# Scan of a two-layer hybrid backbone: row halves issued in turn, one accumulation group for the output, and a step order by tile shape

## The chip, the cores and the metric

One NeuronCore of one Trainium2 chip. The metric is the device time of one execution in microseconds (us): the median of three executions before the change was 3622.27 us (3619.68 to 3623.23).

## The reference, cut to what matters

The program is a two-layer backbone over 1024 latent and 256 context tokens of 1024 channels. The change touches only one stage of layer 0: the two recurrences of the mixer, both in both directions of time.

```python
# eight RWKV-7 heads, state 64x64
S_t = S_{t-1} (diag(w_t) - kk_t (kk_t*a_t)^T) + v_t k_t^T ; y_t = S_t r_t
# four gated DeltaNet heads, state 128x128
S_t = e^{g_t} S_{t-1} + beta_t k_t (v_t - e^{g_t} S_{t-1}^T k_t)^T, o_t = S_t^T q_t
```

Each runs over the context tokens first and then, from that state, over the latent tokens, forwards and backwards. Around it lie the input projection, the output projection, a mixture of experts, and a second layer with windowed attention; all of these stay as they are.

## The kernel before, in words

Time is cut into chunks of 64 tokens, 20 of them (`NCH`), and a step `n` of `Scan.run` (L1142) handles one chunk of both directions and of all heads. All products are fp32, and the trace counts two matmul instructions (with two weight loads) for each product of the program.

Products are small, so each uses only a part of TensorE's 128x128 array. The profile prints that part as rows*columns, and this text calls it the tile shape. Two products in different parts of the array with the same shape can be under way together: in most loops the inner index (`hp`, the half of the heads, or `d`, the direction) selects partitions 0 to 63 or 64 to 127.

A step is made of generators whose pieces ("slices", one per `yield`) are interleaved by the string `ORDER` (L1178), one letter a slice:

- `r`, `rwkv(n)` (L1017): `ps_u` (shape 128*64, L1028), `ps_U` (64*64, L1036), `ps_S` (128*64, L1044), and the output `ps_y` in two slices. The output adds two products for each of 8 units `u`: one with `sv` and `qn` (128*64, L1063) and one with the state `S` (64*64, L1066). They stand one behind the other unit by unit, each unit its own accumulation group.
- `n`, `gdn(n)` (L1077): `ps_ks` and `ps_qs` (128*64, L1096), `ps_Y` (64*64, L1109), the new state `ps_Sg` of each direction in a slice of its own (64*128, L1119), and the output `ps_o` (64*64, L1130).
- `g`, `gram(n+1)` (L945): four slices of `ps_g` (64*128, L964), one for each pair of row half `hp` and direction `d`, each followed by two masks on VectorE (L966 into `ar`, L968 into `qn`); then two slices of transposes `ps_bk` (128*128, L975), copied by ScalarE.
- `c`, `corner(n+1)` (L979): six slices of `ps_p` (32*32, L989, L1003, L1005).

`g` and `c` make matrices of the next step that do not wait for the state. PSUM tiles rotate: three banks for `g` and `c` together (`psg`), two for `r`, three for `n`. TensorE, VectorE and GpSimd run in the order in which the program is written; ScalarE's order is a scheduler's.

The loads of a step come from SyncE's queue in program order: `load2` (L886) brings the channel operands of two steps at once (`ar`, `bk`, `kq`; double buffered), `load_tri` (L912) the inverses of step n+2 (`l21`, `t1`, `TT`), and `load_tok` (L928) the token operands `sv` and `at` of step n+2, behind the last slice of step n, into the buffer of step n. GpSimd gathers `kvtok`, stores `s_y` and `s_o`, and multiplies `dec` and `kd`. At step 6 (`LATER`) the queue also takes the 4 MB of the output projection's weights (`wo_raw`, L1291). In steps 0 and 1, VectorE also finishes a set of inverses (`tri_inv`, L796, L821 and L822), one slice per letter of `ORDER`.

```python
            for i, x in enumerate(ORDER if n else ORDER[1:]):
                if x in g:
                    next(g[x], None)
                if n or i >= TRI0:
                    tri.step(TRI)
```

Of the kernel before, what the change touches and what calls it, by code (L numbers as in the profile page):

```python
# [31 lines left out]
def step_of(m):  # L32
    """Step at which direction 1 meets chunk m, and the chunk of a step."""
    return 3 - m if m < 4 else 23 - m
# [6 lines left out]
def rows_ap(t, off, rows, cols):  # L41
    """rows x cols view of a contiguous DRAM tensor, from element `off`."""
    return bass.AP(tensor=t.tensor, offset=t.offset + off, ap=[[cols, rows], [1, cols]])
# [12 lines left out]
def log_exp_table(K):  # L56
    """Loads the activation table that serves Ln and Exp together."""
    K.table = K.tc.keep_in_program_order(K.nc.scalar.preload_act_table_set("natural_log_exp_and_others")).ins


def behind(K, ins, name):
    """Keeps an instruction behind the named one in program order."""
# [4 lines left out]
def after_table(K, ins):  # L67
    """Keeps an activation behind the last explicit table load."""
# [5 lines left out]
class Fill:  # L74
    """Generators advanced beside a main stream, one slice at a time; lead: instructions they are moved forward."""
# [26 lines left out]
# ---------------------------------------------------------------- constants  # L102
# [4 lines left out]
def consts(K, A):  # L107
# [9 lines left out]
    # per 64-row half: free index minus row index of the half  # L117
# [48 lines left out]
    # silu(c), silu(c_ctx) as [128 d, k, 32] stationaries with two live columns  # L166
# [6 lines left out]
# ---------------------------------------------------------------- ada modulation  # L173
def ada_part(K, A, layer, jj, wp, pp, wtag="adaw", ptag="adap", bufs=2):
    """N-chunks 4jj..4jj+3 of layer's modulation rows: rows 32g (lat), 32g+1 (ctx) of modr[:, jj]."""
# [37 lines left out]
def modcol(K, layer, m, kt, s):  # L213
    """[128,1] column of modulation m for channels 128kt.., stream s (0 lat, 1 ctx)."""
    g = (m % 2) * 2 + kt // 4
    return K.modT[layer][:, m // 2, kt % 4, g, s:s + 1]


def mod_bcast(K, layer, m, s, dst):
    """dst [128, D] <- modulation m of stream s on every partition."""  # L220
# [6 lines left out]
def norm_cols(K, pool, layer, norm, ms, mh, tag):  # L227
    """[128, 2, kt, stream]: gain * (1 + scale), shift of a modulated norm; ms, mh: scale and shift modulations."""
# [11 lines left out]
# ---------------------------------------------------------------- layer-0 input: norm, modulate, transpose  # L240
def head(K, A, hp, hh, hl):
    """hh + hl = modulated RMS norm of [ctx; x], channel layout [128, 8, T]."""
# [61 lines left out]
# ---------------------------------------------------------------- layer-0 projection, column tile by column tile  # L304
def both(nc, out, ps, func, **kw):
    """Activation of a projected column tile (context, latent) into token order."""
# [4 lines left out]
class InProj:  # L311
    """Projected column tiles (first column, continuation), weights loaded two tiles ahead across runs."""
# [28 lines left out]
    def run(self, posts, fills, drain):  # L341
        """Continues the next tiles with posts; fills: (generators, slices per k tile); drain: those to finish."""
# [23 lines left out]
def post_z(K, j, wk, tag, bufs):  # L366
    """Stores the silu of gate tile j."""
# [9 lines left out]
# ---------------------------------------------------------------- RWKV-7 operands  # L377
def store_L(K, unit, n0, x, rev=False):
    """x [(half, s), chunk, t] -> K.s_L [unit, chunk, half, s, t]; chunks n0.. (descending if rev)."""
# [3 lines left out]
class Rwkv:  # L383
    """Token shift, loras, decays and the chunk operands alpha, rho, beta, kappa of both directions.

    With c the running sum of the log decay inside a chunk, in the direction's order:
    alpha = kk e^(c-), rho = r e^c, beta = b e^-c, kappa = k e^-c.
    """
# [26 lines left out]
    def shift(self, ps, j, out):  # L415
        """out = (1 - mu) p + mu/2 (previous + next), zero beyond the ends of each stream."""
# [29 lines left out]
    def invert(self, ct):  # L446
        """Queues the inverses of a column tile once its chunk matrices are traced."""
# [5 lines left out]
    def prep_gen(self, ct):  # L453
# [14 lines left out]
        for bi, (a, m) in enumerate(BLK):  # L468
# [75 lines left out]
            # bonus and gate  # L544
# [28 lines left out]
# ---------------------------------------------------------------- gated DeltaNet operands  # L573
class Gdn:
    """Short convolution, gates and the chunk matrices of the gated delta rule, keys and queries not normalised.

    With nk = 1/|k|: L[t,s] = (k_t.k_s) e^(g_t-g_s) nk_s^2 beta_s, A[t,s] = (q_t.k_s) e^(g_t-g_s) nk_s^2 beta_s,
    r = v/nk - e^g S k, Y = (I+L)^-1 r, o = q S e^g + A Y, S' = e^(gl) S + (k nk^2 beta e^(gl-g))^T Y.
    Rows 0-63 carry direction 0, rows 64-127 direction 1 in flipped token order.
    """  # L580
# [12 lines left out]
    def to_chunks(self, ps, src, w):  # L593
        """ps [(d, p), step, w] <- src [128 token, tile, d, w], direction 1 flipped."""
# [20 lines left out]
    def gates(self, ab):  # L615
# [11 lines left out]
        # softplus(x) = max(x, 0) + ln(1 + e^-|x|)  # L627
# [33 lines left out]
    def conv(self, ps, j):  # L661
        """Five-tap centred convolution over tokens of column tile j."""
# [40 lines left out]
    def sums(self, sq, s, h):  # L703
        """K.ssq[tok, tile, s, h] = sum over channels of the squares, plus eps."""
# [23 lines left out]
    def tok(self, x, h, c0, scaled):  # L728
        """Channel tile x -> token rows of K.s_kv [T, 1024], columns of head h (values divided by nk)."""
# [60 lines left out]
# ---------------------------------------------------------------- inverses of the 32-blocks of I + L  # L790
def inv_blocks(K, c0):
    """The tensor of the inverses of chunk c0, its number of chunks and the place of c0 in it."""
# [1546 lines left out]
```

## Time and profile before

| | us |
|---|---|
| median of three executions | 3622.27 |
| lowest and highest | 3619.68, 3623.23 |
| span of the profiled execution, first to last instruction | 3620.5 |
| TensorE busy in that span | 3343.5 |
| VectorE, ScalarE, GpSimd busy | 2421.4, 2073.4, 731.6 |
| scan, start of step 2 to start of step 19 | 370.45 |

The page gives no separate time of the profiled execution; the median lies 1.8 us above its span. A row of the trace gives start, busy time, engine, line, operation, tiles, and, for a matmul, the tile shape; in square brackets stands the idle time of that engine before it and what ended it. Busy time is the union of a group, and the ends of matmuls are modelled, so the distance from one start to the next tells more than a busy time.

### The profile page before, as it was taken

The page shows a single profiled execution, that of the slowest core. Times are in us where ns is not written, and L with a number is a line of the kernel's source. Part 1 is how long each engine was busy: PE and PEld are TensorE (multiplying, and loading weights), DVE is VectorE, ACT ScalarE, POOL GpSimd, SP SyncE. Part 2 cuts the span into 40 slices and gives each one's busy share as a digit, 9 for nine tenths or more (in the row PEclk, how much of TensorE's full clock was granted, in tenths as well). Part 3 has the DMA queues.
Part 4 walks back from the last instruction along what each step waited for, and adds up shares of the span by engine and source line. Part 5 has one row for each costly group of instructions (what it writes and reads, how often), then busy time and mean ns, then how long its engine had stood idle before and what let it go on. Part 6 is the DMA issues. An engine that isn't in the chain of part 4 may idle for free. (4 is left out here: it accounts for less than half of the span.)

```text
span 3620.5 us, 60293 instructions
## 1 busy us (share of the span) xinstructions
PE 3343.5 (92%) x23392; PEld 2475.0 (68%) x23392; DVE 2421.4 (67%) x4034; ACT 2073.4 (57%) x3529; POOL 731.6 (20%) x716
## 2 busy tenths in 40 slices
PE   5999999996999979699999999899899986999997
PEld 3866667775888867566666666567667764888885
DVE  4267774667343356967777777644666588999998
ACT  4244554332333356376666666453577745888886
POOL 1233322222322244111111100101223310101001
PEclk8999999996999989899999999999699997999998
DMA  5255565666897756468888887663311138999995
GB/s 190 70 190 172 183 204 172 225 187 126 172 210 162 162 167 209 152 245 282 282 288 278 284 286 265 202 230 123 77 39 44 47 110 306 378 396 386 394 375 217
DMA packets 480161, 767.80 MB, mean 212 GB/s; under 512 B 231836, under 2 KB 318532, under 8 KB 472708
## 3 DMA queue, kind: packets, MB, share of 16 engines
q1 hardware_dynamic: 434640, 601.05, 50.2%
q0 software_dynamic: 41648, 151.55, 13.5%
q10 hardware_dynamic: 3587, 11.36, 1.0%
q8 instruction: 184, 3.01, 0.3%
q14 instruction: 102, 0.83, 0.1%
HBM read 631.48 MB, written 132.38 MB: 211 GB/s over the span
## 5 line engine op out<-in xcount | busy, mean ns | idle before, releaser
L1185 DVE TENSOR_TENSOR ulo<-raw,uhi 128x1024 fp32r<-128x1024 f32 x768 | 901.6, 1222 | 127.6 <-ACT uhi L1184 118.9
L1184 ACT ACTIVATE uhi<-raw 128x1024 fp32r<-128x1024 f32 x768 | 789.4, 1069 | 245.2 <-PE ps_y L1624 127.0
L1573 PE MATMUL ps_h<-uhi,xh 128*128 128x512 f32 x1024 | 333.7, 404 | 1.4 <-ACT uhi L1184 1.3
L1573 PE MATMUL ps_h<-ulo,xh 128*128 128x512 f32 x1024 | 320.4, 393 | 3.0 <-DVE ulo L1185 1.0
L1573 PE MATMUL ps_h<-uhi,xl 128*128 128x512 f32 x1024 | 319.0, 392 | 0.0
L1640 POOL DMA_INDIRECT s_x<-yo,idxl x31 | 49.2, 1587 | 977.1 <-DVE yo L1636 977.1
L1573 PEld LDWEIGHTS ps_h<-uhi,xh 128*128 128x128 f32 x1024 | 184.0, 188 | 73.5 <-ACT uhi L1184 21.4
L1573 PEld LDWEIGHTS ps_h<-ulo,xh 128*128 128x128 f32 x1024 | 190.6, 188 | 54.9 <-DVE ulo L1185 12.4
L1573 PEld LDWEIGHTS ps_h<-uhi,xl 128*128 128x128 f32 x1024 | 191.2, 188 | 41.5
L354 PE MATMUL ps_in<-hl,whi 128*128 128x512 f32 x512 | 172.2, 411 | 0.0
L354 PE MATMUL ps_in<-hh,wlo 128*128 128x512 f32 x512 | 169.4, 409 | 1.5 <-POOL wlo L338 1.5
L354 PE MATMUL ps_in<-hh,whi 128*128 128x512 f32 x512 | 169.5, 408 | 0.9 <-DVE convu L671 0.9
L1624 PE MATMUL ps_y<-uhi,th 128*128 128x512 f32 x512 | 167.2, 407 | 0.6 <-ACT tc L1610 0.5
L1624 PE MATMUL ps_y<-ulo,th 128*128 128x512 f32 x512 | 161.1, 395 | 0.1
L1624 PE MATMUL ps_y<-uhi,tl 128*128 128x512 f32 x512 | 158.7, 391 | 0.0
L1910 DVE CUSTOM_DVE_ANT_0 pe<-ps_s,amask,sink 128x640 f32<-128x640 f32 (+2 forms) x128 | 104.4, 816 | 66.7 <-PE ps_s L1903 65.0
L966 DVE TENSOR_TENSOR ar<-ps_g,strict 64x256 f32<-64x256 f32 x80 | 33.8, 422 | 154.2 <-PE ps_g L964 153.9
L1923 POOL TENSOR_SCALAR pe<-pe,ast 128x640 f32<-128x640 f32 (+1 forms) x48 | 92.1, 1919 | 215.1 <-DVE ast L1922 193.7
L1546 ACT ACTIVATE xv<-ps_x,Gf 128x128 f32<-128x128 f32 x256 | 96.7, 471 | 66.7 <-PE ps_x L1542 66.7
L1579 PE MATMUL ps_hc<-raw,xc 128*32 128x512 f32 x1024 | 126.1, 599 | 0.0
L1624 PEld LDWEIGHTS ps_y<-uhi,th 128*128 128x128 f32 x512 | 91.1, 188 | 49.7 <-issue 20.1
L1345 PE MATMUL ps_out<-woh,mh 128*128 128x512 f32 x288 | 117.6, 454 | 0.0
(509 smaller groups left out, 7548.9 us busy)
## 6 DMA issues: line engine op xcount, KB each, us to landing
raw<-in_moe_w_dram SPq DMA_DIRECT2D x384, 1024.0 KB
ada_w<-in_ada_w_dram SPq DMA_DIRECT2D x48, 1024.0 KB
wraw<-in_e_w_in_dram SPq DMA_DIRECT2D x32, 512.0 KB
s_rk<-arbk POOLq DMA_DIRECT2D x16, 1024.0 KB, 5.7
kq<-s_kq SPq DMA_DIRECT2D x20, 512.0 KB
s_x<-ox POOLq DMA_DIRECT2D x18, 512.0 KB
s_h<-ot POOLq DMA_DIRECT2D x18, 512.0 KB, 4.1
s_rkv<-rkv POOLq DMA_DIRECT2D x12, 640.0 KB, 3.9
```

The source lines that it names most:

```text
L354: nc.tensor.matmul(ps, l[:, k, :], r[:, k, a:a + m], start=(k == 0 and n == 0), stop=(k == 7 and n == 2))
L966: nc.vector.tensor_mul(ar[orow, hp, :, cd[d]], pg[orow, :, 0:64], K.strict[orow, d:d + 1, :].to_broadcast([64, 4, 64]))
L1184: K.nc.scalar.activation(hi, src, AF.Copy)
L1185: K.nc.vector.tensor_sub(lo, src, hi)
L1345: nc.tensor.matmul(po[:, cp_], l, r[:, k, c_], start=(k == 0 and n == 0), stop=(k == 7 and n == 2))
L1546: nc.scalar.activation(v[:, q], pt[:, q], AF.Identity, bias=self.nrm[:, 1, k, 0:1], scale=self.nrm[:, 0, k, 0:1])
L1573: nc.tensor.matmul(pl[m][n], l[:, k], r[:, 512 * n:512 * n + 512], start=(k == 0 and i == 0), stop=(k == 7 and i == 2))
L1579: nc.tensor.matmul(pc[32 * g:32 * g + 32], xc[:, k_], rs[g // 2][:, 512 * (g % 2):512 * (g % 2) + 512], start=(k_ == 0), stop=(k_ == 7), s ...
L1624: nc.tensor.matmul(py[n], l[:, k], r[:, 512 * n:512 * n + 512], start=(k == 0 and i == 0), stop=(k == 7 and i == 2))
L1640: nc.gpsimd.indirect_dma_start(out=K.s_x[1], out_offset=bass.IndirectOffsetOnAxis(ap=idx[:, e:e + 1], axis=0), in_=yo, in_offset=None, com ...
L1910: nc.vector.tensor_tensor_reduce(pe[:, a:b], sc[:, 512 - nl + a:512 - nl + b], self.mask[:, m:m + b - a], 1.0, low, OP.add, OP.min, st[:, ...
L1923: (nc.vector if n < NV else nc.gpsimd).tensor_scalar(pes[0][:, :nk], pes[0][:, :nk], st[:, 4, 0:1], None, op0=OP.mult)
```

## The change

Four edits in `Scan`; the comments are also gone, so that line numbers after the change are a few higher (L964 becomes L966, L1063 becomes L1068).

1. `gram`: the products of the two row halves of a direction go in turn into two PSUM banks, in one slice; the masks follow, one half in that slice, the other in the next.
2. `gdn`: the new state of both directions is made in one slice, in turn, in two banks; the two additions on VectorE stay in two slices.
3. `rwkv`: first all products with `sv` (one slice), then all with the state `S` (the next); the whole bank is one accumulation group, in which only unit 0 starts and only unit 7 ends.
4. `ORDER` puts slices of one tile shape behind each other. It has 22 letters as before.

```diff
-        for hp, d in ((0, 0), (1, 0), (0, 1), (1, 1)):
+        H = (slice(0, 64), slice(64, 128))
+        for d in range(2):
             ar, bk, kq = L2[d]
-            pg = self.psg.tile([128, 4, 128], F32, name="ps_g", tag="g")
+            pgs = [self.psg.tile([128, 4, 128], F32, name="ps_g", tag="g") for _ in range(2)]
             for ct in range(4):
-                nc.tensor.matmul(pg[:, ct], ...)
-            nc.vector.tensor_mul(ar[orow, hp, :, cd[d]], pg[orow, :, 0:64], ...)
-            nc.vector.tensor_mul(qn[:, hp, 4 * d:4 * d + 4], pg[:, :, 64:128], ...)
-            yield
+                for hp in range(2):
+                    nc.tensor.matmul(pgs[hp][:, ct], ...)
+            for hp in range(2):
+                orow, pg = H[1 - hp], pgs[hp]
+                nc.vector.tensor_mul(ar[orow, hp, :, cd[d]], pg[orow, :, 0:64], ...)
+                nc.vector.tensor_mul(qn[:, hp, 4 * d:4 * d + 4], pg[:, :, 64:128], ...)
+                yield
...
         for u in range(8):
             for hp in range(2):
-                nc.tensor.matmul(py[H[hp], u], sv[:, hp, u], qn[:, hp, u], start=True, stop=S is None, ...)
-            for hp in range(2) if S is not None else ():
-                nc.tensor.matmul(py[H[hp], u], S[H[hp], u], ..., start=False, stop=True, ...)
-            if u == 3:
-                yield
+                nc.tensor.matmul(py[H[hp], u], sv[:, hp, u], qn[:, hp, u], start=u == 0,
+                                 stop=S is None and u == 7, ...)
+        yield
+        for u in range(8) if S is not None else ():
+            for hp in range(2):
+                nc.tensor.matmul(py[H[hp], u], S[H[hp], u], ..., start=False, stop=u == 7, ...)
...
+        if S2 is not None:
+            pS = [self.psn.tile([128, 4, 128], F32, name="ps_Sg", tag="n") for _ in range(2)]
+            for h in range(4):
+                for d in range(2):
+                    nc.tensor.matmul(pS[d][:, h], kd[H[d], h], Y[H[d], h], start=True, stop=True, ...)
         for d in range(2):
             if S2 is not None:
-                pS = self.psn.tile([128, 4, 128], F32, name="ps_Sg", tag="n")
-                for h in range(4):
-                    nc.tensor.matmul(pS[:, h], kd[H[d], h], Y[H[d], h], start=True, stop=True, ...)
                 ...
             yield
...
-ORDER = "rnrgngrcncngcrcrgngcgc"
+ORDER = "rnrncccrgnngcccrrngggg"
```

In the fences below a row is a line, an operation, its tiles (out<-in) with buffer numbers where several buffers occur, the shape of the output, and a count of equal rows.

TensorE before, in the first half of a step, from the product with the inverses (`ps_U`) to the third gram slice:

```order
L1036 MATMUL ps_U<-up,TT_6898 64x64 x16
L964 MATMUL ps_g<-ar_6910,bk_6911 128x128 x4
L1109 MATMUL ps_Y<-r,TT_6898 64x128 x8
L964 MATMUL ps_g<-ar_6910,bk_6911 128x128 x4
L1044 MATMUL ps_S<-sv,bkt 64x64 x16
L989 MATMUL ps_p<-t_7153,l_7152 32x32 x8
L1119 MATMUL ps_Sg<-Y,kd 128x128 x4
L989 MATMUL ps_p<-TT_6683,l_7152 32x32 x8
L1119 MATMUL ps_Sg<-Y,kd 128x128 x4
L964 MATMUL ps_g<-ar_6920,bk_6921 128x128 x4
```

TensorE with the change, the same place:

```order
L1040 MATMUL ps_U<-up,TT_6683 64x64 x16
L1114 MATMUL ps_Y<-r,TT_6683 64x128 x8
L993 MATMUL ps_p<-t_7476,l_7475 32x32 x8
L993 MATMUL ps_p<-TT_6709,l_7475 32x32 x8
L993 MATMUL ps_p<-t_7476,l_7475 32x32 x8
L1048 MATMUL ps_S<-sv,bkt 64x64 x16
L966 MATMUL ps_g<-ar_7483,bk_7484 128x128 x8
L1124 MATMUL ps_Sg<-Y,kd 128x128 x8
```

The two gram slices of the first direction have moved from either side of `ps_Y` into one run behind `ps_S`, with the state products of both directions behind them; three corner slices stand together.

TensorE before, at the end of a step: the last of the eight pairs of output products (seven equal pairs stand ahead of it), up to the next step's `ps_u`:

```order
L1063 MATMUL ps_y<-qn,sv 64x64 x2
L1066 MATMUL ps_y<-ar_6920,S 64x64 x2
L964 MATMUL ps_g<-ar_6920,bk_6921 128x128 x4
L1130 MATMUL ps_o<-Y,at 64x128 x8
L975 MATMUL ps_bk<-ident,bk_6911 128x128 x4
L1003 MATMUL ps_p<-pm,t_7153 32x32 x8
L975 MATMUL ps_bk<-ident,bk_6921 128x128 x4
L1005 MATMUL ps_p<-TT_6683,pm 32x32 x8
L1028 MATMUL ps_u<-sv,ar_6910 64x64 x8
```

TensorE with the change, the same place, the whole output shown:

```order
L1068 MATMUL ps_y<-qn,sv 64x64 x16
L1073 MATMUL ps_y<-ar_6910,S 64x64 x8
L1073 MATMUL ps_y<-ar_6920,S 64x64 x8
L1137 MATMUL ps_o<-Y,at 64x128 x8
L966 MATMUL ps_g<-ar_7493,bk_7494 128x128 x8
L979 MATMUL ps_bk<-ident,bk_7484 128x128 x4
L979 MATMUL ps_bk<-ident,bk_7494 128x128 x4
L1032 MATMUL ps_u<-sv,ar_7483 64x64 x8
```

The output is now two runs instead of sixteen pieces, and the gram products of the second direction stand directly ahead of the transposes and of the next step's `ps_u`, which reads their masked result.

VectorE with the change, at the end of a step (before, the first two of these masks stood ahead of the output products of the step):

```order
L1143 TENSOR_TENSOR ost<-ps_o,qs 128x512
L970 TENSOR_TENSOR ar_8665<-ps_g,strict 64x4x64
L972 TENSOR_TENSOR qn<-ps_g,incl 128x256
L970 TENSOR_TENSOR ar_8665<-ps_g,strict 64x4x64
L972 TENSOR_TENSOR qn<-ps_g,incl 128x256
L1035 COPY up<-ps_u 128x512
```

All four masks of the second direction now lie between the step's last gram product and the next step's copy `up`. The orders of GpSimd's and SyncE's queues are the same as before.

## Rows read from the trace of the kernel before

**Rows 1.** The page, section 1: busy time, share and count per engine.

```profile
PE 3343.5 (92%) x23392; PEld 2475.0 (68%) x23392; DVE 2421.4 (67%) x4034; ACT 2073.4 (57%) x3529; POOL 731.6 (20%) x716
```

**Rows 2.** Busy time by stretch: step 1, steps 2 to 18, step 19.

```profile
core 0: us, PE busy (x) PEld busy (x) DVE busy (x) ACT busy (x) POOL busy (x), PEclk, DMA share, GB/s
875.99:921.68 45.69, 35.34 (x377) 30.04 (x377) 28.86 (x73) 9.16 (x16) 9.14 (x10) 0.55 0.71 144
921.68:1292.13 370.45, 359.69 (x6397) 305.00 (x6392) 143.98 (x306) 141.47 (x341) 111.21 (x102) 1.00 0.81 173
1292.13:1303.60 11.47, 11.20 (x230) 9.47 (x224) 1.82 (x5) 5.49 (x16) 2.17 (x2) 1.00 0.12 31
```

**Rows 3.** Timeline of TensorE, first half of a step: start, busy, what.

```profile
1082.12 1.15 PE L1044 MATMUL ps_S<-sv,bkt 128*64 128x64 f32 x32
1083.21 0.44 PE L989 MATMUL ps_p<-t,l 32*32 32x32 f32 x16
1083.58 1.16 PE L1119 MATMUL ps_Sg<-Y,kd 64*128 64x128 f32 x8
...
1085.03 0.82 PE L1119 MATMUL ps_Sg<-Y,kd 64*128 64x128 f32 x5
...
1085.69 0.27 PE L1119 MATMUL ps_Sg<-Y,kd 64*128 64x128 f32 x1
1085.80 0.27 PE L964 MATMUL ps_g<-ar,bk 64*128 64x128 f32 x1
1085.80 0.27 PE L1119 MATMUL ps_Sg<-Y,kd 64*128 64x128 f32 x1
...
1086.67 0.44 PE L989 MATMUL ps_p<-t,l 32*32 32x32 f32 x16
```

**Rows 4.** Timeline of TensorE: two of the step's sixteen output pieces, and the next.

```profile
1087.04 0.34 PE L1063 MATMUL ps_y<-qn,sv 128*64 128x64 f32 x4
1087.31 0.33 PE L1066 MATMUL ps_y<-ar,S 64*64 64x64 f32 x4
1087.57 0.34 PE L1063 MATMUL ps_y<-qn,sv 128*64 128x64 f32 x4
```

**Rows 5.** Timeline of TensorE in step 0: corner slices without another shape between.

```profile
857.68 0.44 PE L989 MATMUL ps_p<-t,l 32*32 32x32 f32 x16
857.95 0.42 PE L989 MATMUL ps_p<-TT,l 32*32 32x32 f32 x16
```

**Rows 6.** Waits, steps 2 to 18, TensorE's own: total us, times, longest.

```profile
PE ps_ks L1096 <- issue: 6.4, 18, 0.4
PE ps_u L1028 <- issue: 4.4, 16, 0.4
```

**Rows 7.** Timeline of VectorE: one of the four mask pairs' first masks.

```profile
1114.50 0.42 DVE L966 TENSOR_TENSOR ar<-ps_g,strict 64x256 f32<-64x256 f32 x1 [5.02 <-PE ps_g L964]
```

**Rows 8.** Timeline of SyncE's queue: end of a round of loads, and the next load.

```profile
1209.12 4.46 SPq L924 DMA_DIRECT2D TT<-s_T  x4
1222.65 2.50 SPq L936 DMA_DIRECT2D sv<-s_v  x4
```

**Rows 9.** Waits of SyncE's queue, steps 2 to 18.

```profile
SPq L936 <- PE ps_y L1063: 54.7, 7, 9.3
```

**Rows 10.** Busy time by stretch: two whole steps, loads in full flow, `wo_raw` landing.

```profile
1183.11:1226.79 43.68, 42.33 (x758) 35.95 (x753) 16.96 (x36) 16.65 (x41) 13.17 (x13) 1.00 0.84 168
1193.00:1203.00 10.00, 10.00 (x161) 8.27 (x161) 3.87 (x8) 2.82 (x5) 1.19 (x2) 1.00 1.27 203
1034.00:1044.00 10.00, 10.00 (x184) 8.78 (x181) 5.64 (x13) 4.63 (x10) 1.04 (x1) 1.00 1.02 409
```

**Rows 11.** Timeline of TensorE in step 1, granted clock 0.50.

```profile
891.19 1.98 PE L1036 MATMUL ps_U<-up,TT 64*64 64x64 f32 x32 [10.03 <-DVE up L1031]
...
907.62 0.48 PE L1063 MATMUL ps_y<-qn,sv 128*64 128x64 f32 x4
908.03 0.48 PE L1066 MATMUL ps_y<-ar,S 64*64 64x64 f32 x4
```

More of the change, by code (lines that the diff above doesn't have):

```diff
@@ L956, in gram @@
         self.opr[n] = (qn, bkt, kd)
-        for hp, d in ((0, 0), (1, 0), (0, 1), (1, 1)):
+        H = (slice(0, 64), slice(64, 128))
+        for d in range(2):
             ar, bk, kq = L2[d]
-            hr = slice(64 * hp, 64 * hp + 64)
-            orow = slice(64 * (1 - hp), 64 * (1 - hp) + 64)
-            pg = self.psg.tile([128, 4, 128], F32, name="ps_g", tag="g")
+            pgs = [self.psg.tile([128, 4, 128], F32, name="ps_g", tag="g") for _ in range(2)]
             for ct in range(4):
-                rhs = ar[hr, 0:3:2, ct, cd[d]] if hp == 0 else ar[hr, 1:3, ct, cd[d]]
-                nc.tensor.matmul(pg[:, ct], bk[hr, ct, cd[d]].rearrange("p s t -> p (s t)"), rhs, start=True, stop=True,
-                                 skip_group_check=True)
-            nc.vector.tensor_mul(ar[orow, hp, :, cd[d]], pg[orow, :, 0:64],
-                                 K.strict[orow, d:d + 1, :].to_broadcast([64, 4, 64]))
-            nc.vector.tensor_mul(qn[:, hp, 4 * d:4 * d + 4], pg[:, :, 64:128],
-                                 K.incl[:, d:d + 1, :].to_broadcast([128, 4, 64]))
-            yield
+                for hp in range(2):
+                    hr = H[hp]
+                    rhs = ar[hr, 0:3:2, ct, cd[d]] if hp == 0 else ar[hr, 1:3, ct, cd[d]]
+                    nc.tensor.matmul(pgs[hp][:, ct], bk[hr, ct, cd[d]].rearrange("p s t -> p (s t)"), rhs, start=True,
+                                     stop=True, skip_group_check=True)
+            for hp in range(2):
+                orow, pg = H[1 - hp], pgs[hp]
+                nc.vector.tensor_mul(ar[orow, hp, :, cd[d]], pg[orow, :, 0:64],
+                                     K.strict[orow, d:d + 1, :].to_broadcast([64, 4, 64]))
+                nc.vector.tensor_mul(qn[:, hp, 4 * d:4 * d + 4], pg[:, :, 64:128],
+                                     K.incl[:, d:d + 1, :].to_broadcast([128, 4, 64]))
+                yield
         for d in range(2):
@@ L1062, in rwkv @@
             for hp in range(2):
-                nc.tensor.matmul(py[H[hp], u], sv[:, hp, u], qn[:, hp, u], start=True, stop=S is None,
+                nc.tensor.matmul(py[H[hp], u], sv[:, hp, u], qn[:, hp, u], start=u == 0, stop=S is None and u == 7,
                                  skip_group_check=True)
-            for hp in range(2) if S is not None else ():
+        yield
+        for u in range(8) if S is not None else ():
+            for hp in range(2):
                 nc.tensor.matmul(py[H[hp], u], S[H[hp], u], L2[u // 4][0][H[hp], 2, u % 4, cd[u // 4]],
-                                 start=False, stop=True, skip_group_check=True)
-            if u == 3:
-                yield
+                                 start=False, stop=u == 7, skip_group_check=True)
         yst = p.tile([128, 2, 4, 64], F32, name="yst", tag="yst", bufs=2)
@@ L1114, in gdn @@
         S2 = p.tile([128, 2, 4, 128], F32, name="Sg", tag="Sg", bufs=2) if n + 1 < NCH else None
+        if S2 is not None:
+            pS = [self.psn.tile([128, 4, 128], F32, name="ps_Sg", tag="n") for _ in range(2)]
+            for h in range(4):
+                for d in range(2):
+                    nc.tensor.matmul(pS[d][:, h], kd[H[d], h], Y[H[d], h], start=True, stop=True,
+                                     skip_group_check=True)
         for d in range(2):
             if S2 is not None:
-                pS = self.psn.tile([128, 4, 128], F32, name="ps_Sg", tag="n")
-                for h in range(4):
-                    nc.tensor.matmul(pS[:, h], kd[H[d], h], Y[H[d], h], start=True, stop=True,
-                                     skip_group_check=True)
                 if Sg is None:
-                    nc.vector.tensor_copy(S2[:, d], pS)
+                    nc.vector.tensor_copy(S2[:, d], pS[d])
                 else:
-                    nc.vector.tensor_add(S2[:, d], pS, dec[:, d])
+                    nc.vector.tensor_add(S2[:, d], pS[d], dec[:, d])
             yield
```

## Prediction

> **What bounds the kernel now.** The page comes first: TensorE is busy 92% of the span and no other engine over 67% [rows 1]. That is an average over many stages, so the next view is busy time by stretch, cut where step 1, step 2 and step 19 of the scan begin [rows 2]. From the start of step 2 to that of step 19 lie 370.45 us and 17 steps, 21.79 us a step. [...] TensorE's order sets the step. Its list of waits has two entries, 6.4 and 4.4 us, both "issue": in these steps it waits for no engine and no load [rows 6].
>
> Is it busy with work, then? The timeline answers by the distances between starts. A run of 32 products with 64 output columns in one tile shape takes 1.09 us (`ps_S`, 1082.12 to 1083.21) [rows 3]. The output `ps_y` issues four products, then four of another shape, and each such piece takes 0.265 us (0.53 for two) [rows 4]. With a fixed price s per change of shape and r per product, s + 32r = 1.09 and s + 4r = 0.265 give r = 0.029 and **s = 0.147 us**. For the other shapes: a corner slice takes 0.37 us between other shapes [rows 3] and 0.27 us behind another corner slice [rows 5], so s is 0.10. A run of 8 products of shape 64*128 takes 1.08 us (1.45 from 1083.58 to 1085.03, less the corner slice of 0.37), and its products follow each other at 0.11 us (1085.69, 1085.80), so s is 0.19 [rows 3].
>
> The timeline also shows row halves sharing the array. At 1085.80 a state product (partitions 64 to 127) and a gram product (partitions 0 to 63) start together, in different banks, and that run of 16 takes 1.64 us (1085.03 to 1086.67), not twice 1.08 [rows 3].
>
> **The change, part by part, per step.** Starts are counted to the next start.
>
> - Output (edit 3): 16 pieces of 0.265 are 4.24 us; two runs of 32 are 2.18. Saved 2.06. `ps_o` then follows in the same shape: 0.15 more. That only unit 0 starts the accumulation adds no instruction.
> - Gram and state products (edits 1, 2): before, three gram runs and one state run of 1.08, and the shared run of 1.64, are 5.96 us. After, if every pair of halves takes the 0.11 of one product: 8 pairs of gram and 8 of state in one run are 0.19 + 16 × 0.11 = 1.95, and the second direction is 0.19 + 8 × 0.11 = 1.07. Saved 2.94.
> - Corner (edit 4): six slices of 0.37 are 2.22; twice three together (0.37 + 2 × 0.27) are 1.82. Saved 0.40.
> - `ps_Y` behind `ps_U`, and the two transposes together: a change of shape less each. Saved 0.29.
> - Copies, masks and stores keep their counts, at no cost to the sum: VectorE and ScalarE have some 8.4 us of work [rows 2] in a step that stays above 14. The queues of GpSimd and SyncE keep their order.
>
> TensorE's step becomes 21.79 − 5.84 = **15.95 us**. One wait is added: the second direction's four masks stand between its products and the next step's `ps_u`, at 0.42 us each [rows 7]. The third must end before the second half of `ps_u`, the first two before a bank is free for the second transposes; the two transposes cover 1.0 us of 4 × 0.42. I take 0.5 us (bounds 0 and 1.2). TensorE's step: 16.4.
>
> What is late next: the loads. SyncE's queue brings the loads of two steps in one round, and once a round it waits: from the end of the `TT` loads at 1213.58 to the next issue at 1222.65, 9.1 us [rows 8], for the output products that free `sv` [rows 9]. With the output earlier that wait goes, so the round of 43.68 us can fall to 34.6, or 17.3 us a step. That is the upper bound of the loads' price; the lower comes from the DMA share: two steps carry 43.68 × 0.84 = 36.7 us of packet time [rows 10], and in full flow the share reaches 1.27, so 28.9 us, 14.4 a step. The loads thus bound the step between 14.4 and 17.3 us, with TensorE's 16.4 inside. Two limits so close hinder each other now and then: I take **16.7 us a step**, nearest to TensorE's own, as there the rows are exact.
>
> [...]
>
> The sum:
>
> - Steps 2 to 18: 17 × (21.79 − 16.7) = 86.5 us saved.
> - `wo_raw`: 8 × 512 KB at the 409 GB/s of its stretch [rows 10] are 10.3 us of load time, which the 9.1 us of the queue's wait now hide. Without that cover between 0 and 10.3 come back; I take 5.
> - Step 1 runs at granted clock 0.50 once TensorE has waited 10.03 us for VectorE's inverses [rows 11]; that wait stays, as the inverses do. Behind it the output's pieces take 0.41 us each [rows 11], and a run of 32 is longer by 1.98 / 1.15 [rows 11, 3], so 1.88: 6.56 − 3.76 = 2.8 saved, and for the gram and state products 2.94 × 1.72 = 5.1. VectorE's inverses lie between, so I take 6 of 7.9. Steps 0 and the first grams wait for loads and inverses: nothing.
> - Step 19 has no gram and no corner: 2.2 saved.
>
> Together 86.5 + 6 + 2.2 − 5 = 89.7 us. Nothing behind the scan changes, so all of it should reach the end: span 3620.5 − 89.7 = 3530.8, and with the 1.8 us by which the median lies above the span, **3532.6 us**. A measurement of this kernel can tell about 0.2%, 7 us, from no change.
>
> **The rivals.**
>
> - *The loads bind fully.* Every step waits for SyncE's queue: 17.3 to 18.3 us, and `wo_raw` costs its 10.3. Saved 17 × 4.49 + 8.2 − 10.3 = 74 down to 17 × 3.49 + 8.2 − 10.3 = 57: 3548 to 3565 us. For it speaks how full the queue is already; against it the 1.27.
> - *TensorE alone binds, at less than I take.* No mask wait, and part of the 0.64 us a step of "issue" [rows 6] goes: 15.5 us. Saved 17 × 6.29 + 8.2 = 115: 3507 us.
> - *The halves don't pair* when issued in turn, say because their weight loads hinder each other: 24 pairs cost 24 × 0.11 = 2.6 us more, step 19.0. Saved 17 × 2.79 + 2 = 49: 3573 us. Against it stand the two starts at 1085.80 [rows 3].
> - *The clock falls (slower).* A TensorE that waits for loads may be granted the low clock. In step 1, after an idle time of 10.03 us, the mean clock of the step is 0.55 [rows 2], and a run takes 1.72 times as long though TensorE is then busy [rows 11]. A step of 16.4 would be 28.2 us. It decides from 46% of the steps at the low clock, 17 × (0.46 × 28.2 + 0.54 × 16.4) = 370; with 60% the loss is 17 × 1.7 = 29, less 8: 3643 us. Against it: in two whole steps TensorE now stands 1.35 us of 43.68 [rows 10] without losing the clock, and the load wait I expect is under 1 us a step. [...]
> - *It doesn't do what it says:* the time between shapes is the pipeline's, paid anyway, and nothing changes: 3622 us. The corner slices of step 0 speak against it [rows 5].
>
> **How the numbers follow.** Forecast (16.0 to 17.2 a step) 0.45, loads fully binding 0.25, TensorE alone 0.15, halves not paired 0.07, clock 0.05, no effect 0.03. Slower by over 0.2% is most of the clock rival, 0.04; within 0.2% is no effect and the rest of the clock, 0.04; faster 0.92. The range takes in the first three, whole: from 3498 (a step of 15.0, saving 124) to 3570 (18.6).
>
> **What would show it.** The `ps_y` runs should take 1.09 us each, gram runs of 16 some 1.1, corner slices 0.27, with gram products of both halves starting together. The step should be 16 to 17 us from `ps_u` to `ps_u`; SyncE's wait for `ps_y` should shrink to little, and TensorE's waits should name a load (of `ar`, `bk` or the inverses) or the masks. The forecast is wrong if the granted clock leaves 1.00 in steps 3 to 18, if ScalarE or VectorE is named as TensorE's releaser for more than 1 us a step, or if the stages behind the scan grow by what the scan gives.

## The result and the profile after

The changed kernel takes **3555.85 us** (median of 4 runs, 3550.13 to 3562.51), beside 3622.68 us before (4 runs, 3619.68 to 3623.23). The ratio is 0.982, with a 95% interval of 0.9802 to 0.9838. The change saves 66.8 us where 89.7 were forecast: inside the range, 23 us above the time forecast, among the times that one of the rivals gave. All ratios here are of fast runs; one slow run of the old order, 3742 us at a granted clock of 0.82, is left out.

Section 1 of the page after, and busy time by stretch (step 1, steps 2 to 18, step 19), which answer to [rows 1, 2]:

```profile
PE 3235.4 (91%) x23392; PEld 2395.0 (67%) x23392; DVE 2419.9 (68%) x4034; ACT 2073.3 (58%) x3529; POOL 732.1 (21%) x716
```

```profile
core 0: us, PE busy (x) PEld busy (x) DVE busy (x) ACT busy (x) POOL busy (x), PEclk, DMA share, GB/s
871.64:902.81 31.17, 17.64 (x376) 15.62 (x377) 29.59 (x73) 9.84 (x21) 6.71 (x7) 0.78 1.02 184
902.81:1220.68 317.87, 273.18 (x6393) 243.45 (x6392) 138.68 (x306) 141.70 (x341) 114.88 (x106) 0.95 0.94 204
1220.68:1230.10 9.42, 9.15 (x225) 8.36 (x224) 1.82 (x5) 4.37 (x10) 2.20 (x2) 1.00 0.11 35
```

The instructions are the same in number. Steps 2 to 18 fall from 370.45 to 317.87 us (52.6 saved), step 1 from 45.69 to 31.17 (14.5), step 19 from 11.47 to 9.42 (2.1); what follows the scan keeps its length within 1.5 us. But TensorE, busy 97% of steps 2 to 18 before, is now busy 86%, its granted clock is 0.95 instead of 1.00, and the DMA share is 0.94 instead of 0.81.

The pieces themselves came out as the working priced them. TensorE's timeline of step 10, one of the steps with no wait but the masks' (15.49 us from `ps_u` to `ps_u`), beside [rows 3, 4]:

```profile
1064.16 0.44 PE L993 MATMUL ps_p<-t,l 32*32 32x32 f32 x16
1064.43 0.42 PE L993 MATMUL ps_p<-TT,l 32*32 32x32 f32 x16
1064.69 0.42 PE L993 MATMUL ps_p<-t,l 32*32 32x32 f32 x16
1065.04 1.15 PE L1048 MATMUL ps_S<-sv,bkt 128*64 128x64 f32 x32
1066.12 1.16 PE L966 MATMUL ps_g<-ar,bk 64*128 64x128 f32 x16
1067.11 1.06 PE L1124 MATMUL ps_Sg<-Y,kd 64*128 64x128 f32 x16
1068.10 0.34 PE L1009 MATMUL ps_p<-TT,pm 32*32 32x32 f32 x10
...
1068.79 1.15 PE L1068 MATMUL ps_y<-qn,sv 128*64 128x64 f32 x32
1069.88 1.15 PE L1073 MATMUL ps_y<-ar,S 64*64 64x64 f32 x32
1070.86 1.04 PE L1137 MATMUL ps_o<-Y,at 64*64 64x128 f32 x16
...
1074.04 0.63 PE L979 MATMUL ps_bk<-ident,bk 128*128 128x128 f32 x4 [0.46 <-DVE qn L972]
1074.59 0.63 PE L1032 MATMUL ps_u<-sv,ar 128*64 128x64 f32 x14
```

The reader is to see, from start to start: a run of 16 gram products of both halves in 0.99 us (as the trace counts them) and one of 16 state products in 0.99, the output in 1.09 and 0.98, corner slices at 0.27, and the mask wait of 0.46 that the working took as 0.5. What holds the other steps is in TensorE's list of waits, steps 2 to 18, here its eight longest entries (it had two before, [rows 6]):

```profile
PE ps_p L993 <- DMA t<-s_T: 9.7, 1, 9.7
PE ps_bk L979 <- DVE qn L972: 7.4, 16, 0.6
PE ps_p L1007 <- issue: 6.2, 3, 3.0
PE ps_p L993 <- DMA TT<-s_T: 5.2, 6, 1.3
PE ps_y L1068 <- issue: 4.2, 3, 1.8
PE ps_p L993 <- issue: 3.9, 4, 1.3
PE ps_p L1009 <- issue: 3.1, 2, 1.7
PE ps_u L1032 <- DMA sv<-s_v: 1.9, 2, 1.7
```

Three kinds stand there: loads that are late (`t`, `TT`, `sv`), the masks, and "issue", in which the profile names nobody. SyncE's queue shows the longest wait of the first kind, and TensorE the step it cost (29.3 us):

```profile
1007.35 5.35 SPq L1298 DMA_DIRECT2D wo_raw<-in_e_w_out_dram  x8
...
1013.78 8.51 SPq L920 DMA_DIRECT2D t<-s_T  x1
1022.33 4.95 SPq L924 DMA_DIRECT2D TT<-s_T  x4
```

```profile
1027.18 0.64 PE L993 MATMUL ps_p<-t,l 32*32 32x32 f32 x16 [9.65 <-DMA t<-s_T]
...
1029.37 1.98 PE L1048 MATMUL ps_S<-sv,bkt 128*64 128x64 f32 x32
1031.28 2.08 PE L966 MATMUL ps_g<-ar,bk 64*128 64x128 f32 x16
```

Behind the 4 MB of `wo_raw` one `t` load takes 8.51 us to issue (median of the program's 20: 0.86); TensorE waits 9.65 us and then runs at a granted clock of 0.50 up to 1035.27 (a run of 32 in 1.91 instead of 1.09 us).

As the prediction said, SyncE's wait for `ps_y` [rows 9] is gone. Its largest wait in steps 2 to 18 is now this one, and all of them together are 30 us of 317.87:

```profile
SPq L936 <- ACT sv L1061: 5.0, 2, 4.2
```

What goes with "issue", the trace's DMA records tell. Section 3 of the page lists a queue named "instruction" with 184 packets of 16 KB:

```profile
q8 instruction: 184, 3.01, 0.4%
```

They are read here as fetches of TensorE's own instructions, because the counts fit: TensorE has 254 matmuls and weight loads for each over the program (46784 on 184) and 251 in steps 2 to 18 (12785 on 51, three a step). Those of the other engines don't: VectorE has 22 and 6 instructions for each, ScalarE 19 and 7, GpSimd 4 and 2. Where TensorE stops for "issue" for long, it goes on 1.2 to 1.8 us after such a fetch has ended. Five of the stops, with the trace's row for the last:

| after the change: TensorE stops | fetch runs | TensorE goes on | behind the fetch's end |
|---|---|---|---|
| 930.50 | 930.66 to 931.91 | 933.54 | 1.63 |
| 967.45 | 967.09 to 968.59 | 969.83 | 1.24 |
| 1051.33 | 1050.30 to 1051.63 | 1053.07 | 1.44 |
| 1086.00 | 1085.02 to 1086.09 | 1087.71 | 1.62 |
| 1125.01 | 1123.67 to 1125.19 | 1126.76 | 1.57 |

```profile
1126.76 1.23 PE L1068 MATMUL ps_y<-qn,sv 128*64 128x64 f32 x26 [1.75 <-issue]
```

In steps 2 to 18 of this run and of the nine others below that keep the change's order and edits, 101 waits of over 0.5 us are put down to "issue", and all of them end 1.2 to 1.8 us behind a fetch. From here on an idle time of over 0.1 us that ends 1.1 to 1.8 us behind a fetch's end is counted as "late instructions". Fetches come 6 us apart on average, so such a count takes in about one wait in nine by chance. Of TensorE's 44.6 us of idle time in steps 2 to 18, 19.9 are of this kind, 7.3 are masks, and 14.9 are other waits of the corner slices, mainly for `t` and `TT`.

### The profile page after: what moved, and what is told of

Same layout as the page of the kernel before. It is cut to its first block, busy times and chain, and to the rows that moved or that the text cites. A ratio compares the mean times of both kernels' runs of the same rounds, so it can differ in the third digit from the quotient of the medians.

```text
span 3548.4 us, 60256 instructions
## 1 busy us (share of the span) xinstructions
PE 3235.4 (91%) x23392; PEld 2395.0 (67%) x23392; DVE 2419.9 (68%) x4034; ACT 2073.3 (58%) x3529; POOL 732.1 (21%) x716
## 3 DMA queue, kind: packets, MB, share of 16 engines
q0 software_dynamic: 41648, 151.55, 13.8%
## 5 line engine op out<-in xcount | busy, mean ns | idle before, releaser
L821 DVE TENSOR_TENSOR invt<-invB,invX 128x112 f32<-128x112 f32 (+27 forms) x248 | 93.1, 375 | 29.1 <-DMA invB<-s_L 24.0
```

The source lines that it names most:

```text
L821: nc.vector.tensor_mul(t, B[:N, k, k + 1:, None].to_broadcast([N, r, c]), X[:N, k, None, 0:c].to_broadcast([N, r, c]))
```

## The experiments

All short diffs are against the changed kernel unless the text says otherwise. The table holds what their profiles show of steps 9 to 18 (ten whole steps, `wo_raw` not among them except at the end of the versions that load it late), idle times in us over the ten; the sections behind it say what each was for. Longer pieces, compact, and loads nobody reads also have `wo_raw` late. The last three kernels compute on old operands, so their output is not the reference's, and each ran once. Any wait that ends behind a fetch is counted with the late instructions, also one that the profile names otherwise (1.7 us for `sv` in the change, masks); the 17.4 us of the old order hold 1.9 that the profile calls "issue", in the same place and not behind a fetch. Small waits of other kinds, 2 us at most, and the 6.6 us of "issue" in the kernel before, of which none ends so, are not in it.

| kernel | ratio to before (95%) | us a step | DMA share | idle: late instructions | idle: loads | idle: masks |
|---|---|---|---|---|---|---|
| before | 1 | 21.8 | 0.73 | 0 | 0 | 0 |
| order alone | 0.9948 (0.9919 to 0.9977) | 18.8 | 0.84 | 0.7 | 0 | 0 |
| old order | 0.9897 (0.9877 to 0.9918) | 19.2 | 0.88 | 0.4 | 17.4 | 0 |
| the change | 0.9820 (0.9802 to 0.9838) | 17.9 | 0.92 | 10.5 | 4.7 | 4.5 |
| the change again | 0.9828 (0.9806 to 0.9849) | 18.1 | 0.97 | 11.6 | 3.4 | 4.6 |
| `wo_raw` late | 0.9825 (0.9807 to 0.9843) | 18.2 | 0.97 | 11.2 | 4.4 | 3.8 |
| `wo_raw` late, again | 0.9802 (0.9770 to 0.9833) | 18.7 | 0.97 | 13.2 | 6.1 | 3.2 |
| two queues | 0.9817 (0.9792 to 0.9842) | 18.1 | 0.93 | 14.4 | 0 | 4.0 |
| longer pieces | 0.9781 (0.9756 to 0.9807) | 17.9 | 0.98 | 15.9 | 0 | 2.7 |
| compact | 0.9798 (0.9779 to 0.9818) | 17.9 | 0.96 | 13.8 | 0 | 4.1 |
| no loads | one run | 15.2 | 0.24 | 0 | 0 | 4.6 |
| half the loads | one run | 15.6 | 0.54 | 0 | 0 | 4.6 |
| loads nobody reads | one run | 17.3 | 0.96 | 12.6 | 0 | 3.2 |

**The loads left out.**

```
 def load_tri(self, n):   (load2, load_tok alike)
+    if n >= 8:
+        self.tri[n] = (self.tri_tile(n),) + self.tri[6 + n % 2][1:]
+        return
```

> This kernel is the change with the loads of SyncE left out from step 8 of the scan on (row halves' operands, triangles, values, at tiles): later steps compute on the operands of steps 4 to 7 that are still in memory, so its output is not the reference's; the gathers of POOL and all arithmetic stay. Theory (the loads set the step since the change): from step 9 on every step takes what TensorE alone needs, 15.2 to 15.7 us, with the granted clock at 1.00 and no 18.8 us steps; the scan from step 9 to step 18 is some 25 to 30 us shorter than after the change. Rival one (TensorE's own chain, the masks of VectorE and the states, sets it): the steps stay at 17 us or more, still alternating. Rival two (the low clock is a cause, not a consequence of the waits): stretches at half clock remain in steps 9 to 18.

Measured: every step from 8 to 18 takes 15.2 us. Busy time by stretch, steps 9 to 18, and TensorE's only wait there:

```profile
1026.70:1178.72 152.02, 147.47 (x3760) 133.95 (x3758) 81.01 (x180) 83.22 (x200) 65.58 (x61) 1.00 0.24 72
```

```profile
PE ps_bk L987 <- DVE qn L980: 4.6, 10, 0.5
```

TensorE needs 15.2 us with its masks. Neither the masks nor VectorE hold it longer, and the clock stays at 1.00 through ten pauses of 0.46 us: the low clock after the change comes with its longer waits and is not there without them.

**`wo_raw` behind step 17.**

```
-LATER = 6
+LATER = 17
```

> The change, with the 4 MB load of the output weights (wo_raw) issued behind step 17 of the scan instead of step 6, when the scan has no more loads of its own to make. Theory (the loads are the bound in the middle of the scan, so 4 MB more of them cost a step about their own time): the step of 29.3 us becomes 17 to 19, and the whole is 9 to 12 us faster than after the change, about 3539 to 3549 us, if the weights still arrive before the products behind the scan ask for them. Rival (the long step is the chance of one late triangle, and the queue catches up later): under 4 us faster. If the weights come late for what follows the scan, part of the gain is lost there: the stretch behind the scan would be longer than 2316.9 us.

Measured: the long step is gone (20.7 us in place of 29.3), steps 2 to 18 take 306.3 us in place of 317.9, and what follows the scan is no longer than before. But the kernel before took 3603 us in this comparison and not 3622, so the ratio, 0.9825, shows no gain. Hence a second time, with the change itself beside it:

> The change itself, unaltered, beside the others of this call, since the kernel before took 3622 us on one chip and 3603 on another. Its ratio to the kernel before should again be 0.980 to 0.984, with steps 2 to 18 at 18 to 19 us on average, alternating between 15.2 to 15.5 and longer ones, and one step near 29 us where wo_raw lands.

> The change with wo_raw behind step 17, once more, so that it stands beside the change on one chip. In its first trace no step of 29 us was left, and the 17 steps took 306.3 us against 317.9 after the change, on another chip. Theory (4 MB more in a full queue cost a step about their own time): 9 to 12 us faster than the change here. Rival (the queue catches up): within 4 us of it.

Here the change takes 3558.8 us and the late version 3545.5: 13 us less by the medians, but the intervals of the ratios overlap (0.9806 to 0.9849 and 0.9770 to 0.9833). The step of 28 us (change) is 18.2 us (late). But steps 2 to 18 as a whole differ by only 4.3 us in these two traces (314.1 and 309.8; 11.6 in the first pair), and 13.0 of the 16.3 us between the two spans lie ahead of step 0 of the scan (857.02 and 843.98), where the edit moves no load. That the wait goes is shown; what it is worth, 4 to 12 us by these traces, is not settled.

**The old order of the slices.**

```
-ORDER = "rnrncccrgnngcccrrngggg"
+ORDER = "rnrgngrcncngcrcrgngcgc"
```

> The change with the old order of the slices: halves in turn and the one accumulation group of the output stay, corner slices and joins go back to the old places. By the prices of the prediction TensorE's step grows by the corner's 0.40 and the joins' 0.29 us, to about 16 us. Theory (loads set the step at about 18): no more than 4 us slower than the change, for the extra TensorE time lies beside the loads' waits: 3550 to 3560. Rival (TensorE's instructions still set the step): 19 steps of 0.7 us, 13 us slower, about 3565 to 3570.

Measured: ratio 0.9897 against 0.9820, so 28 us of 3603 are lost, more than either expectation (which counted from 3622) allowed. TensorE's best steps are 15.8 us, 0.6 above the 15.2 of the change, as priced. The rest is waiting, and the granted clock behind the waits, 0.91 on average over steps 9 to 18 where the change has 0.97. The waits of steps 2 to 18:

```profile
PE ps_g L966 <- DMA bk<-s_rk: 24.6, 12, 5.2
PE ps_p L993 <- DMA t<-s_T: 4.3, 1, 4.3
```

The old order asks for the first gram products right behind `ps_U`, 3.9 us into the step, the new one behind `ps_S` and three corner slices, 7.0 us into it. Which operand is late went with the order: `bk` here, `t` and `TT` in the change (9.7 and 5.2 us in steps 2 to 18). Hardly an instruction is late here in steps 9 to 18 (0.4 us).

**The new order alone, on the kernel before.**

```
-ORDER = "rnrgngrcncngcrcrgngcgc"
+ORDER = "rnrncccrgnngcccrrngggg"
```

> The kernel before with only the new order of the slices. By the prices of the prediction TensorE's step of 21.8 us falls by 0.69 (corner 0.40, joins 0.29), to 21.1, still far above the loads' 17 to 18, so that all of it shows: 19 steps of 0.69 are 13 us, about 3610 us. Theory: 3605 to 3613. Rival (the order does nothing by itself, all gain comes from the halves): within 4 us of 3622. If the order also takes masks off TensorE's way or adds waits for them, it is 5 us off on either side.

Measured: 0.9948, so 19 us of 3603 by the ratio, more than the theory's 9 to 17, but the runs spread from 3557 to 3606 us. The profiled run (3572 us) has steps of 18.7 us, not 21.1:

```profile
1054.20:1242.60 188.40, 187.66 (x3761) 165.34 (x3761) 81.59 (x180) 82.59 (x201) 64.98 (x59) 1.00 0.84 173
```

Start to start, one step of either trace: corner slices 1.57 instead of 2.22 us, gram and state products 5.06 instead of 6.0 (slices of one shape that follow each other pair by themselves: the last two gram slices, 16 products, take 1.64 instead of twice 1.08), and the "issue" waits of [rows 6], 0.64 a step, are gone. These are 2.2 of the 3.1 us. The parts of the change are thus no sum: halves in turn take the same pairing as the order does.

The spread of the runs goes with the granted clock: over a whole run it was 0.949 at 3557 us, 0.943 at 3572, and 0.934 and 0.932 at the two of 3605 to 3606. The trace shows one such loss. In step 8, behind the load of `wo_raw`, TensorE waits for `t` (and, shortly after, twice for `TT`, 0.57 and 0.26 us), and then the clock is at 0.50 for 20.5 us; the step takes 31.0 us instead of 18.7:

```profile
1030.40 0.44 PE L989 MATMUL ps_p<-t,l 32*32 32x32 f32 x16 [2.36 <-DMA t<-s_T]
```

```profile
1031.84:1052.32 20.48, 20.41 (x233) 17.85 (x234) 5.06 (x9) 4.21 (x11) 2.36 (x4) 0.50 1.06 188
```

Whether it is this step that differs from run to run isn't known, since one run of the ten is traced.

**Two queues.**

```
-self.last = nc.sync.dma_start(l21, ...)      (and t1, TT)
+self.last = nc.scalar.dma_start(l21, ...)
```

> The change with the six loads of a step's triangles and inverses (4608 pieces of 128 B of the 10368 pieces of a step) issued by ScalarE instead of SyncE, so that two queues carry the scan's loads. Theory A (one queue hands out its pieces too slowly, the DMA engines themselves have room): the step falls from 18 to 15.5 to 16.5 us, the mean DMA share rises above 1.0, 25 to 40 us faster than the change. Theory B (the DMA engines' own time per piece is the limit, whoever issues): within 5 us of the change, share as before, 0.92 to 0.97. A loss is possible in either if ScalarE's copies stand behind an issue that waits for a free tile: then TensorE's waits name ScalarE.

Measured: 3557.7 us beside 3558.8, theory B. Something else moved, though. The waits for `t` and `TT` are gone, and the late instructions have taken their place (27.6 us in steps 2 to 18, 19.9 after the change). SyncE's queue now has time to spare, 53.8 us of 180.6 in steps 9 to 18, and the step is no shorter for it:

```profile
SPq L936 <- PE ps_y L1068: 53.8, 7, 12.2
```

**Fewer, longer pieces.**

```
-K.s_L = dt("s_L", (12, NCH, 2, 64, 64))
+K.s_L = dt("s_L", (NCH, 2, 64, 12, 64))
-ar = p.tile([128, 3, 4, 2, 64], ...)
+ar = p.tile([128, 4, 2, 4, 64], ...)
```

> The change with wo_raw behind step 17 and with fewer, longer pieces: the triangles lie in memory with the 12 units side by side, so that a load of them is 128 runs of 3 KB instead of 1536 of 128 B (twice the bytes, the unused half comes along), and alpha and rho of a row half come as runs of 512 B instead of two of 256 B. Pieces per two steps fall from 20736 to 15872. Theory A (the number of pieces sets the queue's time): 18 us a step times 0.77 is 13.8, below TensorE's 15.2, so TensorE sets the step: 15.3 to 15.8, 40 to 45 us faster than the late version in steps 2 to 18. Theory B (the pieces' own time sets it): by the trace a piece of 128 B takes 13 ns, one of 256 B 23, one of 512 B 34 and one of 4 KB some 200; the triangles gain nothing, alpha and rho 1.4 us a round, so 0.7 us a step at most: 0 to 12 us faster than the late version.

Measured: 3542.3 us beside 3545.5 of the late version: theory B, a quarter fewer pieces buy nothing that can be told. Here no load is late any more, and TensorE still needs 17.9 us a step. Its longest waits, steps 2 to 18:

```profile
PE ps_y L1068 <- issue: 12.4, 6, 3.7
PE ps_p L1007 <- issue: 6.0, 3, 4.6
PE ps_bk L979 <- DVE qn L972: 5.9, 13, 0.5
PE ps_p L1009 <- issue: 3.9, 5, 1.9
PE ps_p L993 <- issue: 2.8, 4, 1.2
```

28.1 of its 36.4 us of idle time end behind a fetch. That made a new theory: the loads hold TensorE not only by its operands but by its instructions, if those are what the 16 KB packets bring.

**Loads that nobody reads.** The products take old operands, as with the loads left out, but SyncE issues every load, into other memory:

```
+if m >= 4:
+    ar, bk, kq = self.dm[f"ar{d}"], self.dm[f"bk{d}"], self.dm[f"kq{d}"]
-self.ld[m] = d_
+self.ld[m] = d_ if m < 4 else self.ld[2 + m % 2]
```

> Which of two prices of the loads is paid: operands that come late, or instructions that come late. The traces so far show TensorE's own instructions fetched by DMA in blocks of 16 KB, and most of its idle times behind step 1 (19.9 of 44.6 us after the change, 28.1 of 36.4 in the version with fewer pieces) end 1.1 to 1.8 us after such a fetch has ended. Here, from step 8 on, SyncE still issues every load of the scan, but into memory that nothing reads, and the products use the operands of steps 6 and 7 or of the rounds 2 and 3 that lie there (output not the reference's; wo_raw behind step 17). No product can wait for a load then. Fetch theory: the idle times that end behind a fetch stay, 0.8 to 2 us a step, and steps 9 to 18 are 16 to 17.2 us as long as SyncE's loads still flow at a DMA share near 0.9 or more, 15.2 only where they have run out. Rival (late operands are the price): 15.2 to 15.5 in every step, as when the loads were left out.

Measured: 17.3 us a step, just above what the fetch theory gave, and far from 15.2. Busy time by stretch and the longest of TensorE's waits from step 9 to 18:

```profile
1023.10:1195.62 172.52, 156.26 (x3761) 139.82 (x3761) 81.56 (x180) 83.31 (x200) 65.80 (x61) 0.97 0.96 204
```

```profile
PE ps_bk L986 <- DVE qn L979: 4.1, 9, 0.5
PE ps_y L1075 <- issue: 3.9, 2, 2.7
PE ps_S L1055 <- issue: 3.7, 2, 3.4
PE ps_p L1016 <- issue: 2.0, 1, 2.0
PE ps_y L1080 <- issue: 1.5, 1, 1.5
```

No load is waited for, yet 2.0 us a step are lost. This run also gives the loads' pace when nothing holds SyncE: it never waits, and its rounds begin at 983.83, 1020.28, 1056.90, 1095.49, 1133.21 and 1170.31 us: 37.3 us a round, **18.6 us a step**, at a share of 0.96. That is not a floor. In the change, whose SyncE waits 11 us in steps 9 to 18, the rounds behind `wo_raw` begin at 1035.46, 1070.32, 1107.03, 1143.65 and 1179.53: 36.0 a round, 18.0 a step.

**Half of the loads.**

```
 def load2(self, m):
+    if m >= 4:
+        self.ld[m] = self.ld[2 + m % 2]
+        return
```

> From step 8 on only the loads of the row halves' operands (ar, bk, kq: 9216 of the 20736 pieces of two steps, nearly half of the packet time) are left out, those of rounds 2 and 3 are used again (output not the reference's); triangles, inverses, values, at tiles and gathers stay. The DMA share should fall from 0.92 to about 0.6. Fetch theory: below a share of some 0.7 no fetch is late, so 15.2 us a step with only the mask wait of 0.46 left. Rival (the triangles' 128-byte pieces are what comes late, whatever else flows): waits for t and TT stay, steps of 16 us and more.

Measured: 15.5 to 15.8 us in every step from 9 on, share 0.54, clock 1.00, and no wait but the masks. The rival falls: the 128-byte pieces are in time when the other loads don't flow.

**A candidate, compact.**

```
-nc.sync.dma_start(kq..., dap(K.s_kq[d], m * 128, [[8 * T, 128], [T, 8], [1, 128]]))
+nc.sync.dma_start(kq..., dap(K.s_kq[d], m * 131072, [[1024, 128], [1, 1024]]))
```

> A candidate for a faster kernel: wo_raw behind step 17, alpha and rho in runs of 512 B instead of two of 256 B, and the keys and queries (kq) laid out in memory so that a partition's run is 4 KB instead of eight of 512 B. By the trace's times per piece this takes 1.3 and 1.4 us a round off the 34.4 us of packet time. If late fetches and late operands both grow with the packet time in flow, a step gains some 0.5 to 1.4 us, 8 to 24 us in all against the late version (ratio to the kernel before 0.973 to 0.979). Rival, as in the version with wide triangles: the queue only runs closer to TensorE, idle time moves from operands to fetches, and the ratio stays at 0.978 to 0.983. The stores of kq before the scan become 512-byte pieces; if that costs there, the scan starts later than at 834 us.

Measured: 0.9798, as the rival has it: again no load late, again 17.9 us a step. The scan begins no later. The versions with `wo_raw` late end at 0.978 to 0.983; the one with longer pieces is the best of them. Which of them is truly ahead of the change, and by how much, these runs don't tell.

## Why the prediction was right, and where it was not

- **Output, halves, corner, masks: right.** TensorE's own step was to be 15.95 us plus 0.5 for the masks; it is 15.2 with them. The difference is mostly the 0.64 us of "issue" [rows 6], which the working left in its base and which went (the rival of 15.5 had it), and corner slices of 1.57 us a step instead of 1.82. Only the runs without their loads show this step throughout.
- **The loads' price: the term that was too small.** The working bounded the loads by 14.4 and 17.3 us a step and took 16.7 for the step, 0.3 above what it gave TensorE alone. Steps 2 to 18 took 18.7 on average, 18.0 without the long one, where TensorE alone needs 15.2: some 3 us instead of 0.3. In part the rounds are longer. The upper bound was SyncE's round of 43.68 us less its wait of 9.1 [rows 8], 34.6; with the change a round took 36.0 us, and 37.3 with loads nobody reads. In the shorter step the gathers and stores of GpSimd come closer together too (share of their queue in steps 9 to 18 0.19 instead of 0.16); whether that slows SyncE's loads is not shown. The lower bound was the share of 1.27 in 10 us of full flow [rows 10]. A burst is not a rate: over ten steps no version here got above 0.98. In part the path was another: the working asked only when operands arrive, and 2.0 us a step are lost where no product waits for a load (loads nobody reads).
- **`wo_raw`: 5 us taken, some 11 paid in its step** (29.3 us beside 18.0), about the upper bound of 10.3. Loaded late, it gave 4 to 12 us back.
- **The rival "the loads bind fully"** gave 3548 to 3565 us and a step of 17.3 to 18.3, with a chance of 0.25 against 0.45. Its number is the one that came, its mechanism only in part. Its 18.3 is half of the 36.7 us of packet time [rows 10], so it takes a DMA share of 1 for the end. No run shows 1 as a limit: over ten steps the share was 0.98 at most, at 17.9 us a step (longer pieces), and over 10 us it was 1.27. The rival had every step wait for SyncE's queue; but steps of 15.2 to 16 us stand among those of 17 to 22, more of the idle time in steps 9 to 18 is late instructions (10.5 us) than late operands (4.7), and with time to spare in SyncE's queue (two queues) the step stays as long (18.1 us beside 17.9). So the measured time lies in the stated range because the range took in a rival whose path was half right: that much is luck.
- **The clock rival came in part, and with it a sign that the prediction had named for being wrong:** that the granted clock leaves 1.00 in steps 3 to 18. In steps 2 to 18 it is at 0.50 in six stretches, 34.1 us together. TensorE is busy 27.4 us of them. If all its work there slows like the run of 32 behind the late `t` load, 1.91 instead of 1.09 us, it would have needed 15.6 at 1.00, so by this estimate some 12 us are lost. The rival had 46% of the steps there; it is 11% of their time. The rows below are one of the six: soon behind the pause of 1.75 us the clock was 0.50 for 3.4 us, then back. The pauses of 1.73 and 1.71 us (rows three and four of the table of fetches) left it at 1.00. Over steps 2 to 18 TensorE's 15.2 us would make 258.7; 317.87 were taken. Of the 59.2 more, 37.3 are idle time beside the masks, some 12 the low clock, and some 10 are neither. Part of these 10 is there without any wait: with half of the loads, at clock 1.00 and with the masks as the only wait, a step takes 15.6 us.

```profile
1126.76:1127.40 0.64, 0.64 (x21) 0.64 (x23) 0.00 (x0) 0.00 (x0) 0.00 (x0) 1.00 0.51 110
1127.40:1130.80 3.40, 3.40 (x56) 3.28 (x54) 0.00 (x0) 0.60 (x1) 0.00 (x0) 0.50 0.48 119
1130.80:1132.00 1.20, 1.20 (x22) 1.03 (x20) 0.61 (x1) 0.00 (x0) 1.17 (x2) 0.98 1.12 178
```

- **Step 1: 6 us taken, 14.5 saved.** Before, the low clock behind VectorE's inverses lasted nearly to the end of the step [rows 2, 11]; now it ends within 6 us of TensorE's going on at 887.16. The order alone (33.0 us) and the old order with halves and output (32.0) each give it, so either is enough. Why the clock comes back sooner is not shown.

```profile
887.16:890.00 2.84, 2.83 (x43) 2.84 (x45) 2.74 (x9) 0.73 (x2) 0.43 (x1) 0.50 1.07 303
890.00:893.00 3.00, 3.00 (x86) 2.63 (x86) 2.79 (x7) 1.82 (x4) 0.61 (x1) 0.68 1.34 193
893.00:896.00 3.00, 3.00 (x94) 2.77 (x90) 2.83 (x8) 0.49 (x2) 0.00 (x0) 1.00 0.81 90
```

The sum as it came out: steps 2 to 18 gave 52.6 us where 81.5 were forecast with `wo_raw`, 28.9 less; step 1 gave 8.5 more; step 19 as forecast. That is 20 of the 23 us between forecast and result. The profiled runs differ by a few us ahead of the scan, too: its step 0 begins at 856.60 before and at 851.78 after.

## What to carry to other kernels

Price a bound that comes next by its rate over whole rounds, with the other queues at their new pace, not by its best 10 us: here that was 16.7 against 18 us a step, and the difference was most of what was missing. When one engine gets faster, look at everything it draws through the DMA engines, its instructions too: after the change late instructions cost 10.5 us in ten steps and late loads 4.7. Taking loads away and then letting them flow unread told the two prices apart (15.2 and 17.3 us a step beside 17.9). And the order of the products can be a choice of which load may be late: `bk` in the old order here, `t` and `TT` in the new.

## What the hardware showed that was not expected

- The DMA records have a queue "instruction" with packets of 16 KB, 1.2 us each on average in steps 2 to 18 and one for some 250 instructions of TensorE. TensorE's "issue" waits of over 0.5 us, 101 in ten runs, all end 1.2 to 1.8 us after such a fetch. With the loads taken out no wait ends so in steps 9 to 18; at a share of 0.54 none either, at 0.84 two in ten steps, at 0.92 and above eight or more. Only the count by share is shown; how the fetches stand in line is not.
- Longer pieces made no step shorter: 17.9 us at 224 GB/s (the unused half of the triangles counted in) beside 18.1 us at 198 GB/s in the change run again and 17.3 at 204 with loads nobody reads. `wo_raw` lands at 409 [rows 10]. In steps 9 to 18 of the change a piece of 128 bytes takes 13 ns on average, one of 256 bytes 23 and one of 512 bytes 34, so a longer piece takes longer, and the pieces' times add up to a share of 0.92 to 0.98. What else limits these loads, and how a share can reach 1.27 for 10 us, stays open.
- TensorE's granted clock kept 1.00 through pauses of 0.46 us in every step and through two of 1.7; it was 0.50 for 3.4 us soon behind one of 1.75, and for 20.5 us behind one of 2.36 and two short ones (order alone). The length of a pause by itself thus did not tell what followed.
